# NSA attention of a fused two-layer network: mask on TensorE, exponential from PSUM, a pinned order two head pairs ahead

## The chip, the cores and the metric

The kernel runs on one core of a Trainium2 chip. TensorE (PE, with its weight loads PEld) multiplies matrices out of SBUF into PSUM; VectorE (DVE), ScalarE (ACT) and GpSimd (POOL) work on tiles; SyncE (SP) issues most of the DMAs. Each engine takes its instructions in the order of its own queue, and semaphores make one wait for another. The metric is the device time of one execution in microseconds (us).

## The reference, cut to what matters

The program is a network of width 1024 over 256 tokens: a mixer with retention and mLSTM, a feed-forward block, a gated embedding, then the NSA mixer (native sparse attention), a second feed-forward block and embedding, and two hybrid attention blocks. The change is in the NSA mixer, and in helpers that the hybrid blocks share with it. With 256 tokens all four selection blocks are selected and the window of 512 covers everything, so that the selected and the window branch are two causal attentions over all 256 keys, with keys and values of their own. What is computed per head and query:

```python
s = jnp.einsum('bghqd,bgnd->bghqn', qq, kc) * scale        # compressed branch: 15 block keys
p_c = jnp.where(cvalid, jax.nn.softmax(jnp.where(cvalid, s, NEG), axis=-1), 0.0)
o_cmp = jnp.einsum('bghqn,bgnd->bghqd', p_c, vc)
s = jnp.where(smask, einsum(qq, kg) * scale, NEG)          # selected branch
o_slc = einsum(softmax(s), vg)
s = jnp.where(wmask, einsum(qq, kwb) * scale, NEG)         # window branch
o_win = einsum(softmax(s), vwb)
return g[..., 0:1] * o_cmp + g[..., 1:2] * o_slc + g[..., 2:3] * o_win   # then @ w_out
```

There are 16 heads of 64 in two groups of 8; a group shares its keys and values.

## The kernel before, in words

Tokens stand in two blocks of 128 (`tb`), heads in pairs (`e` is the head in the pair), and a pair holds both branches (`b`: 0 selected, 1 window). There are eight pairs, four of each group.

The projections multiply fp32 by fp32 in three fp32r matmuls (`mm3`, L485 to L487): each operand is split into a high and a low half. `wt` loads a weight tile by SP, ACT casts the high half (L468, `whi`) and DVE takes the rest (L469, `wlo`), with four buffers of each kind. `nat` (L502) is a projection of 1024 columns deep, 512 wide, for both token blocks: 96 matmuls for two output halves, 48 for one query group.

The NSA stage goes: normalised input turned, compressed keys' and values' inputs, keys and values, gates, `compress(0)`, the queries of group 0 (`qgroup(0)`: projection, norm, query turn L1158), `compress(1)`, `qgroup(1)`, then `attention(0)` and `attention(1)`, then `nsa.out`, the output projection, which ends with the addition to the residual.

`attention` first does the compressed branch of the group, token block by token block: 4 small matmuls (L1172), a softmax of 9 DVE operations (L1178 to L1188) with one ACT exponential, a transpose (L1190) and a copy into `cT`. Then for each pair: per token block the scores `s4` (L1204), one matmul per head for both branches; per head and branch one DVE custom operation (L1207) that adds the mask, writes the masked scores to SBUF with their sign turned and takes the row extreme; the exponential on ACT from SBUF to SBUF with the row sum (L1209); reciprocal, gate, and 4 multiplications of the probabilities on DVE per token block (L1211 to L1216). `pv_pair` then transposes the probabilities, three 128x128 blocks into one PSUM bank (L703), copies them to a `pT` tile (ACT L708 or DVE L706), and multiplies with the values (L711, L714) onto the compressed part (L1218). The result is split into `xh` (ACT, L1222) and `xl` (DVE, L1223), the input of `nsa.out`.

PSUM has eight banks: three of `acc`, two of `sc`, two of `tp`, one of `po`. The order of the instructions on each engine is set by a scheduler that simulates the program as written and takes what is ready; in the stage before the change PE's order here is the scheduler's. `pinned()` (L436), used by the hybrid blocks, fixes PE's order to that in which the code is written; `high_priority` lets an operation go ahead of others in the scheduler's choice. A generator used as `fill` gives single steps of other work between.

Of the kernel before, what the change touches and what calls it, by code (L numbers as in the profile page):

```python
# [8 lines left out]
F32 = mybir.dt.float32  # L9
# [6 lines left out]
P = 128  # L16
# [357 lines left out]
class Builder:  # L374
# [318 lines left out]
    def pv_pair(self, po, p0, p1, v, ns, start):  # L693


        nc = self.nc
        for s in range(ns):
            pts = []
            for e in range(2):
                tp = self.pt.tile([P, 512], F32, tag="tp", name=self.nm("tp"))  # L700
                a0, a1 = p0(e, s), p1(e, s)
                for j, a in enumerate((a0, a1[:, 0:P], a1[:, P:T])):
                    nc.tensor.transpose(tp[:, j * P:(j + 1) * P], a, self.ident)  # L703
                pT = self.ph.tile([P, 384], F32, tag="pT", bufs=3, name=self.nm("pT"))
                if e:
                    nc.vector.tensor_copy(pT, tp[:, :384])  # L706
                else:
                    nc.scalar.activation(pT, tp[:, :384], AF.Copy)  # L708
                pts.append(pT)
            for e in range(2):  # L710
                nc.tensor.matmul(po[e * 64:e * 64 + 64, :], lhsT=v(s, 0, e), rhs=pts[e][:, 0:T],  # L711
                                 start=start and s == 0, stop=False)
            for e in range(2):
                nc.tensor.matmul(po[e * 64:e * 64 + 64, P:T], lhsT=v(s, 1, e), rhs=pts[e][:, T:384],  # L714
                                 start=False, stop=s == ns - 1)
# [287 lines left out]
    def nsa(self):  # L1003
# [56 lines left out]
        for b in range(2):  # L1060
            tp = self.pt.tile([P, 2, T], F32, tag="tp", name=self.nm("tp"))
            for g in range(2):
# [8 lines left out]
              for n, tags in (("k", [(a + b, 1) for b in "01" for a in ("qn", "qT")]),  # L1071
                              ("v", [("pr1", 2), ("pr1", 2), ("w1", 2), ("w1", 2)]))]
# [67 lines left out]
        def qgroup(g):  # L1140
            acc = self.nat(f"nsa.q{g}", xs, 8)
            qn = self.ph.tile([P, 2, 8, 64], F32, tag=f"qn{g}", name="qn")
            qT = self.ph.tile([P, 4, T], F32, tag=f"qT{g}", name="qT")
            a3 = lambda tb: acc[tb].rearrange("p (h d) -> p h d", d=64)
            for tb in range(2):
                if tb:
                    nc.scalar.activation(qn[:, tb], a3(tb), AF.Copy)
                else:
                    nc.vector.tensor_copy(qn[:, tb], a3(tb))
            qf = self.sm.tile([P, 2, 8], F32, tag="qf", name=self.nm("qf"))  # L1150
            head_factor(a3, 8, qf, 0.125)
            for tb in range(2):
                tt(qn[:, tb], qn[:, tb], qf[:, tb].unsqueeze(2).to_broadcast([P, 8, 64]), op=ALU.mult)
            for k0 in range(0, 4, 2):
# [6 lines left out]
                nc.scalar.activation(qT[:, k0:k0 + 2, :], tp, AF.Copy, scale=V("nsa_qg"))  # L1161
# [4 lines left out]
        def attention(g, qT):  # L1166

            cT = ph.tile([P, T], F32, tag="cpT", bufs=1, name="cpT")
            for tb in range(2):
                sp = self.psc.tile([P, 512], F32, tag="sc", name=self.nm("sc"))  # L1170
                for pr in range(4):
                    nc.tensor.matmul(sp[:, pr * 32:pr * 32 + 32], lhsT=qT[:, pr, tb * P:(tb + 1) * P], rhs=kc[:, g],  # L1172
                                     start=True, stop=True)
                e = ph.tile([P, 8, 16], F32, tag="ce", bufs=2, name=self.nm("ce"))
                mx = self.sm.tile([P, 8], F32, tag="cmx", name=self.nm("cmx"))
                fc = self.sm.tile([P, 8], F32, tag="cfc", name=self.nm("cfc"))
                b16 = lambda a: a.unsqueeze(2).to_broadcast([P, 8, 16])
                tt(e, sp[:, 0:128].rearrange("p (h n) -> p h n", n=16),  # L1178
                   c("nsa.cmask")[:, tb * 16:tb * 16 + 16].unsqueeze(1).to_broadcast([P, 8, 16]), op=ALU.add)
                nc.vector.tensor_reduce(mx, e, AX.X, ALU.max)  # L1180
                ts(mx, mx, -1e20, None, ALU.max)
                tt(e, e, b16(mx), op=ALU.subtract)
                nc.scalar.activation(e, e, AF.Exp)
                nc.vector.tensor_reduce(fc, e, AX.X, ALU.add)
                ts(fc, fc, 1e-30, None, ALU.max)
                nc.vector.reciprocal(fc, fc)
                tt(fc, fc, gate[:, tb, g * 8:g * 8 + 8, 0], op=ALU.mult)
                tt(e, e, b16(fc), op=ALU.mult)  # L1188
                tp = self.pt.tile([P, 2, T], F32, tag="tp", name=self.nm("tp"))
                nc.tensor.transpose(tp[:, 0, 0:P], e.rearrange("p h n -> p (h n)"), self.ident)  # L1190
                nc.scalar.activation(cT[:, tb * P:(tb + 1) * P], tp[:, 0, 0:P], AF.Copy)
            for pr in range(4):
                p1 = ph.tile([P, 2, 2, T], F32, tag="pr1", bufs=2, name=self.nm("pr1"))
                p0 = ph.tile([P, 2, 2, P], F32, tag="pr0", bufs=2, name=self.nm("pr0"))
                nm = self.sm.tile([P, 2, 2, 2], F32, tag="nm", name=self.nm("nmx"))
                l = self.sm.tile([P, 2, 2, 2], F32, tag="l", name=self.nm("l"))
                for tb, pt in ((1, p1), (0, p0)):
                    nk = P * (tb + 1)
                    banks = 2 if tb else 1
                    sps = [self.psc.tile([P, 512], F32, tag="sc", name=self.nm("sc")) for _ in range(banks)]  # L1200
                    for e in range(2):
                        hs = slice(e * 64, e * 64 + 64)
                        s4 = (sps[e] if tb else sps[0][:, e * 256:e * 256 + 256]).rearrange("p (b k) -> p b k", b=2)
# [7 lines left out]
                    nc.vector.reciprocal(l[:, tb], l[:, tb])  # L1211
                    hd = g * 8 + 2 * pr
                    tt(l[:, tb], l[:, tb], gate[:, tb, hd:hd + 2, 1:3], op=ALU.mult)
# [657 lines left out]
```

## Time and profile before

| | us |
|---|---|
| median of 3 runs | 1415.21 |
| lowest and highest | 1412.82, 1420.18 |
| profiled execution | 1417.63 |
| its span (first to last instruction) | 1415.8 |
| granted clock, mean over the span | 0.988 |

The profile is of one execution. Its busy times count an engine as busy while an instruction of it runs; since instructions overlap a little at their ends, the sum of single durations is larger than the busy time of their stretch. Times in the text are us from the start of the span. A granted clock of 1.00 is TensorE's level of 2.4 GHz and 0.50 is that of 1.2 GHz. Some matmul and other records are missing from the trace, so counts in a stretch fall short of those in the program by some per cent. The NSA stage runs from about 360 to 518.

### The profile page before, as it was taken

Reading aid. Unit: us, or ns where it says so; the run is one execution under the profiler, and the core shown is the slowest. Engines: PE = TensorE matmul, PEld = TensorE weight load, DVE = VectorE, ACT = ScalarE, POOL = GpSimd, SP = SyncE. Lnnn points to the kernel's source line nnn. Section 1 sums busy time; section 2 is a strip of 40 time slices with the busy share of each in tenths; the row PEclk is TensorE's granted clock in tenths of the full one; section 3 lists DMA queues with packets and bytes.
Section 4 is the critical chain, followed back from the end, with each engine's and each line's share of the span. In section 5 each row is a group of like instructions: output and inputs, shape, how many; then the busy total and the mean of one; then the engine's idle time right before and its main releaser. Section 6 shows DMA issues by size and latency. Waiting matters only on the chain. (4 is left out here: it accounts for less than half of the span.)

```text
span 1415.8 us, 23842 instructions
## 1 busy us (share of the span) xinstructions
PE 1371.8 (97%) x9029; PEld 1196.3 (84%) x9029; DVE 1019.5 (72%) x2215; ACT 761.0 (54%) x1383; POOL 70.9 (5%) x108
## 2 busy tenths in 40 slices
PE   8999999999899999999999999999999999999997
PEld 8777999888765589998779898997879998997886
DVE  6777889887777778888587777555577767546467
ACT  6355656536455656554365656445555555545443
POOL 0000000003000000000030202000000201000000
PEclk9999999999997999999999999999999999999999
DMA  6444667896640047668754444453665544554562
GB/s 246 149 144 158 183 228 242 294 332 221 226 150 16 28 152 238 213 234 315 242 169 155 150 148 136 158 172 116 196 205 171 151 137 127 158 184 133 171 194 75
DMA packets 74759, 251.90 MB, mean 178 GB/s; under 512 B 10578, under 2 KB 14162, under 8 KB 74516
## 3 DMA queue, kind: packets, MB, share of 16 engines
q1 hardware_dynamic: 68880, 239.87, 50.9%
q0 software_dynamic: 4272, 7.17, 2.3%
q10 hardware_dynamic: 1492, 3.34, 0.8%
q8 instruction: 71, 1.16, 0.3%
q14 instruction: 44, 0.36, 0.1%
HBM read 248.42 MB, written 1.90 MB: 177 GB/s over the span
## 5 line engine op out<-in xcount | busy, mean ns | idle before, releaser
L469 DVE TENSOR_TENSOR wlo<-raw,whi 128x1024 fp32r<-128x1024 f32 (+2 forms) x386 | 461.6, 1199 | 212.6 <-ACT whi L468 211.9
L468 ACT ACTIVATE whi<-raw 128x1024 fp32r<-128x1024 f32 (+2 forms) x386 | 399.3, 1036 | 330.5 <-PE acc L487 146.9
L485 PE MATMUL acc<-xh,whi 128*128 128x256 f32 (+1 forms) x1360 | 390.1, 288 | 7.5 <-ACT xh L601 5.0
L486 PE MATMUL acc<-xl,whi 128*128 128x256 f32 (+1 forms) x1360 | 386.0, 284 | 0.3 <-DVE xl L602 0.3
L487 PE MATMUL acc<-xh,wlo 128*128 128x256 f32 (+1 forms) x1360 | 385.0, 283 | 0.5 <-DVE wlo L469 0.5
L485 PEld LDWEIGHTS acc<-xh,whi 128*128 128x128 f32 (+1 forms) x1360 | 258.7, 191 | 14.9 <-ACT xh L601 6.0
L486 PEld LDWEIGHTS acc<-xl,whi 128*128 128x128 f32 (+1 forms) x1360 | 259.4, 191 | 1.9 <-DVE xl L602 1.1
L487 PEld LDWEIGHTS acc<-xh,wlo 128*128 128x128 f32 (+1 forms) x1360 | 259.3, 191 | 1.7 <-DVE wlo L469 0.8
L485 PE MATMUL acc<-whi,xh 128*128 128x512 f32 (+2 forms) x688 | 251.5, 367 | 2.0 <-ACT xh L601 0.8
L487 PE MATMUL acc<-whi,xl 128*128 128x512 f32 (+2 forms) x688 | 248.8, 363 | 1.4 <-DVE xl L602 1.4
L486 PE MATMUL acc<-wlo,xh 128*128 128x512 f32 (+2 forms) x688 | 247.9, 361 | 0.0
L485 PEld LDWEIGHTS acc<-whi,xh 128*128 128x128 f32 x688 | 130.0, 189 | 24.6 <-ACT xh L601 2.2
L487 PEld LDWEIGHTS acc<-whi,xl 128*128 128x128 f32 x688 | 129.9, 189 | 22.4 <-DVE xl L602 2.6
L486 PEld LDWEIGHTS acc<-wlo,xh 128*128 128x128 f32 x688 | 130.1, 189 | 18.7 <-issue 1.7
L485 PE MATMUL acc<-whi,gh 128*128 128x512 f32 x176 | 70.3, 399 | 0.0
L486 PE MATMUL acc<-wlo,gh 128*128 128x512 f32 x176 | 69.5, 395 | 0.0
L487 PE MATMUL acc<-whi,gl 128*128 128x512 f32 x176 | 69.4, 394 | 0.0
L1526 POOL DMA_DIRECT2D bias<-brow x48 | 29.2, 635 | 448.2 <-DVE nmx L1551 157.6
L625 ACT ACTIVATE sqj<-h 128x512 f32<-128x512 f32 (+1 forms) x40 | 23.5, 587 | 48.8 <-DVE h L1783 16.3
L1333 DVE CUSTOM_DVE_ANT_0 adw<-adw,ada 128x1024 f32<-128x1024 f32 x32 | 39.1, 1221 | 13.1 <-DMA adw<-weights 13.1
L951 DVE SCALAR_TENSOR_TENSOR cy<-zp,vecs,cy 128x256 f32<-128x256 f32 x88 | 42.2, 480 | 0.8
L485 PEld LDWEIGHTS acc<-whi,gh 128*128 128x128 f32 x176 | 33.1, 188 | 8.1 <-issue 0.5
(423 smaller groups left out, 1871.2 us busy)
## 6 DMA issues: line engine op xcount, KB each, us to landing
raw<-weights SPq DMA_DIRECT2D x384, 512.0 KB, 3.9
adw<-weights SPq DMA_DIRECT2D x48, 512.0 KB, 4.8
bias<-brow POOLq DMA_DIRECT2D x48, 128.0 KB, 3.8
w<-weights SPq DMA_DIRECT2D x8, 512.0 KB, 7.7
raw<-weights SPq DMA_DIRECT2D x8, 416.0 KB, 3.7
const_ab<-consts SPq DMA_DIRECT2D x1, 1536.0 KB, 6.9
h<-x SPq DMA_DIRECT2D x4, 256.0 KB, 4.5
gb<-rows ACTq DMA_DIRECT2D x2, 512.0 KB, 5.1
```

The lines of the kernel that those rows point to most:

```text
L468: nc.scalar.activation(hi, r, AF.Copy)
L469: nc.vector.tensor_tensor(lo, r, hi.bitcast(F32), op=ALU.subtract)
L485: mm(out, lhsT=a[0], rhs=b[0], start=start, stop=False)
L486: mm(out, lhsT=a[0], rhs=b[1], start=False, stop=False)
L487: mm(out, lhsT=a[1], rhs=b[0], start=False, stop=stop)
L625: self.nc.scalar.activation(j, src, AF.Square, scale=2048.0 ** -0.5, accum_out=dst)
L951: stt(y, az[:, k:k + T], V(f"ffn_cw{i}", k * 22 + j), y, ALU.mult, ALU.add)
L1333: nc.vector.tensor_tensor_reduce(raw, raw, cr, 1.0, 0.0, ALU.mult, ALU.add, m[:, j:j + 1])
L1526: nc.gpsimd.dma_start(b3[:, g], bass.AP(b0.tensor, b0.offset + ((4 * qd + 2 * pr + e) * 3 + g) * 384 + 127, [[24 * 384 - 16, 8], [24 * 384 ...
```

## The change

In the NSA stage:

- The mask is added by TensorE: `idr`, an identity, and `tri`, the 128x128 triangle of the mask, both cast to fp32r on ACT once. Four matmuls of `idr` with `tri` a pair add to the diagonal blocks of the scores in PSUM. Two casts on ACT are new, with a wait for the NSA constants.
- DVE takes the row maximum of each score bank with one `tensor_reduce` per head and token block (four a pair), and ACT takes the exponential straight from PSUM into the probability tile `pr` (three buffers). The custom operation is gone.
- The scores of both heads of a pair stand next to each other on PE, those of token block 0 in two `acc` banks.
- The probabilities are transposed and copied back in place (`turn_block`), and all value matmuls of a pair come together (`pv_all`); both were helpers of the hybrid blocks and are now shared. Their copies there now have priority.
- The compressed branch takes both token blocks in one bank, with ten DVE operations a group, eight of them of double width.
- The query projection is split: `q_in` (first token block 0, then 1), `q_norm`, `q_turn`. Its second group's second token block is filler around the first pairs' scores; the query turn of group 1 comes between pairs.
- PE's order from the query turn of group 0 to the last pair is pinned: the scores of pair n+2 come ahead of the transposes of pair n.

The diff, cut to its core:

```diff
+    def turn_block(self, a, on_vector):
+        tp = self.pt.tile([P, 512], F32, tag="tp", name=self.nm("tp"))
+        for j in range(3):
+            nc.tensor.transpose(tp[:, j * P:(j + 1) * P], a[:, j * P:(j + 1) * P], self.ident)
+        with self.tc.high_priority(offset=200):
+            if on_vector:
+                nc.vector.tensor_copy(a, tp[:, :384])
+            else:
+                nc.scalar.activation(a, tp[:, :384], AF.Copy)
+    def pv_all(self, items, start=True):
+        mm = self.nc.tensor.matmul
+        for n, (po, pts, v) in enumerate(items):
+            for e in range(2):
+                mm(po[e * 64:e * 64 + 64, :], lhsT=v(0, e), rhs=pts[e][:, 0:T], start=start and n == 0, stop=False)
...
-                        nc.tensor.matmul(s4, lhsT=qT[hs, pr, tb * P:(tb + 1) * P], rhs=kT[hs, g, :, 0:nk],
-                                         start=True, stop=True)
-                        for b in range(2):
-                            nc.vector.tensor_tensor_reduce(pt[:, e, b], s4[:, b], mask[:, T - nk:], -1.0, 3e38, ALU.add,
-                                                           ALU.min, nm[:, tb, e, b:b + 1])
-                            nc.scalar.activation(pt[:, e, b], pt[:, e, b], AF.Exp, scale=-1.0, bias=nm[:, tb, e, b:b + 1],
-                                                 accum_out=l[:, tb, e, b:b + 1])
...
+        idr, tri = [ph.tile([P, P], F32R, tag=t, name=t) for t in ("idr", "tri")]
+        nc.scalar.activation(idr, self.ident, AF.Copy)
+        nc.scalar.activation(tri, mask[:, P:T], AF.Copy)
+        def scores(g, pr, qT):
...
+            for tb in (1, 0):
+                nk = P * (tb + 1)
+                for e in range(2):
+                    hs = slice(e * 64, e * 64 + 64)
+                    nc.tensor.matmul(sps[tb][e], lhsT=qT[hs, pr, tb * P:(tb + 1) * P], rhs=kT[hs, g, :, 0:nk],
+                                     start=True, stop=False)
+            for tb in (1, 0):
+                for e in range(2):
+                    nc.tensor.matmul(sps[tb][e][:, :, P * tb:P * tb + P], lhsT=idr,
+                                     rhs=tri.unsqueeze(1).to_broadcast([P, 2, P]), start=False, stop=True)
+            for tb in (1, 0):
+                o, nk = P * tb, P * (tb + 1)
+                for e in range(2):
+                    nc.vector.tensor_reduce(nm[:, tb, e], sps[tb][e], AX.X, ALU.max, negate=True)
+                    for b in range(2):
+                        nc.scalar.activation(pp[:, e, b, o:o + nk], sps[tb][e][:, b], AF.Exp, bias=nm[:, tb, e, b:b + 1],
+                                             accum_out=l[:, tb, e, b:b + 1])
...
+        self.take(q_in(0, qn[0]), 9)
+        q_norm(0, qn[0])
+        fill = q_in(1, qn[1])
+        compress(1)
+        self.take(fill, 4)
+        with self.pinned():
+            qT, cT = [q_turn(0, qn[0])], []
+            self.take(fill, 1)
+            es = compressed(0, qT[0])
+            pps = [scores(0, 0, qT[0])]
+            self.take(fill, 2)
+            pps.append(scores(0, 1, qT[0]))
+            self.take(fill, 2)
+            with self.tc.high_priority(offset=200):
+                q_norm(1, qn[1])
+            cT.append(compressed_turn(es))
+            for n in range(8):
+                g, pr = divmod(n, 4)
+                if n < 6:
+                    pps.append(scores((n + 2) // 4, (n + 2) % 4, qT[(n + 2) // 4]))
+                if n == 1:
+                    qT.append(q_turn(1, qn[1]))
+                values(g, pr, pps.pop(0), cT[g], fill)
+                if n == 1:
+                    es = compressed(1, qT[1])
+                if n == 2:
+                    cT.append(compressed_turn(es))
```

How the order of the engines changes is shown at three places. On PE in the loop over pairs, before (`sc` are score banks, `tp` the transposes' banks, `po` the output bank, `pr_802` and `pr_803` the two probability tiles of one pair):

```order
L1204 MATMUL sc_4916<-kT,qT 128x512
L703 MATMUL tp_4835<-const_g,pr_803_4795 128x128
L703 MATMUL tp_4835<-const_g,pr_802_4794 128x128 x2
L703 MATMUL tp_4841<-const_g,pr_803_4795 128x128
L703 MATMUL tp_4841<-const_g,pr_802_4794 128x128 x2
L1204 MATMUL sc_4917<-kT,qT 128x512
L711 MATMUL po_4833<-pT_4839,vsw 64x256
L711 MATMUL po_4833<-pT_4845,vsw 64x256
L714 MATMUL po_4833<-pT_4839,vsw 64x128
L714 MATMUL po_4833<-pT_4845,vsw 64x128
L703 MATMUL tp_4851<-const_g,pr_803_4795 128x128
L703 MATMUL tp_4851<-const_g,pr_802_4794 128x128 x2
```

The scores of later banks stand singly between transposes and value matmuls of the pair before, and each branch's values follow its transposes at once. On PE in the same loop in the changed kernel (`acc` are here the score banks of token block 0):

```order
L1234 MATMUL sc_4953<-kT,qT 128x512
L1234 MATMUL sc_4954<-kT,qT 128x512
L1234 MATMUL acc_4951<-kT,qT 128x256
L1234 MATMUL acc_4952<-kT,qT 128x256
L1238 MATMUL sc_4953<-tri,idr 128x2x128
L1238 MATMUL sc_4954<-tri,idr 128x2x128
L1238 MATMUL acc_4951<-tri,idr 128x256
L1238 MATMUL acc_4952<-tri,idr 128x256
L704 MATMUL tp_4987<-const_g,pr_4801 128x128 x3
L704 MATMUL tp_4992<-const_g,pr_4801 128x128 x3
L704 MATMUL tp_4997<-const_g,pr_4801 128x128 x3
L704 MATMUL tp_5002<-const_g,pr_4801 128x128 x3
```

All four score matmuls and the four mask matmuls of a pair stand in a block ahead of the twelve transposes of the pair two before, and the eight value matmuls of that pair follow these.

On DVE in the loop over pairs, before (`nmx` the row extremes, `l` the row sums, `pT` the copies of transposed probabilities):

```order
L706 COPY pT_4711<-tp_4707 128x384
L1207 ISA pr_802_4794,nmx_4796<-sc_4798,const_nsa 128x256
L1207 ISA nmx_4796 128x1
L1211 RECIPROCAL l_4722<-l_4722 128x4
L1207 ISA pr_802_4794,nmx_4796<-sc_4798,const_nsa 128x256
L1207 ISA nmx_4796 128x1
L1213 TENSOR_TENSOR l_4722<-l_4722,gate 128x4
L1207 ISA pr_802_4794,nmx_4796<-sc_4799,const_nsa 128x256
L1207 ISA nmx_4796 128x1
L1216 TENSOR_SCALAR pr_787_4720<-pr_787_4720,l_4722 128x128 x3
L1223 TENSOR_TENSOR xl_4198<-po_4683,xh_4197 128x256
L1216 TENSOR_SCALAR pr_787_4720<-pr_787_4720,l_4722 128x128
```

The operations of two pairs are mixed as they become ready. On DVE in the same loop in the changed kernel (`pr` is copied to in place):

```order
L1243 TENSOR_REDUCE nmx_4949<-sc_4953 128x2
L1243 TENSOR_REDUCE nmx_4949<-sc_4954 128x2
L708 COPY pr_4801<-tp_4992 128x384
L1243 TENSOR_REDUCE nmx_4949<-acc_4951 128x2
L1243 TENSOR_REDUCE nmx_4949<-acc_4952 128x2
L708 COPY pr_4801<-tp_5002 128x384
L1247 RECIPROCAL l_4950<-l_4950 128x4
L1249 TENSOR_TENSOR l_4950<-l_4950,gate 128x4
L1253 TENSOR_SCALAR pr_4948<-pr_4948,l_4950 128x256 x4
L1247 RECIPROCAL l_4950<-l_4950 128x4
L1249 TENSOR_TENSOR l_4950<-l_4950,gate 128x4
L1267 TENSOR_TENSOR xl_4198<-po_5007,xh_4197 128x256
```

A pair now takes four maxima, two copies, and two rounds of reciprocal, gate and multiplications; `xl` of the pair that is being finished stands between the second round's gate and its multiplications.

On PE at the start of the attention, before:

```order
L485 MATMUL acc_4413<-whi_4469,xh_3890 128x512
L486 MATMUL acc_4413<-wlo_4470,xh_3890 128x512
L487 MATMUL acc_4413<-whi_4469,xl_3891 128x512
L1111 MATMUL sc_4402<-raw_4400,cmpu_4393 30x64 x2
L1172 MATMUL sc_4527<-kcb,qT 128x32 x4
L1132 MATMUL tp_4407<-vcn,const_nsa 128x64
L1172 MATMUL sc_4548<-kcb,qT 128x32 x4
L1132 MATMUL tp_4407<-vcn,const_nsa 128x64
L1204 MATMUL sc_4573<-kT,qT 128x512
L1204 MATMUL sc_4574<-kT,qT 128x512
L1204 MATMUL sc_4591<-kT,qT 128x256
```

The second query group's 48 matmuls are done ahead of the first score of group 0. On PE at the same place in the changed kernel:

```order
L487 MATMUL acc_4404<-whi_4442,xl_3891 128x512
L1173 MATMUL tp_4455<-const_g,qn 128x128 x4
L1138 MATMUL tp_4399<-vcn,const_nsa 128x64
L1173 MATMUL tp_4461<-const_g,qn 128x128 x4
L485 MATMUL acc_4467<-whi_4406,xh_3890 128x512
L486 MATMUL acc_4467<-wlo_4407,xh_3890 128x512
L487 MATMUL acc_4467<-whi_4406,xl_3891 128x512
L485 MATMUL acc_4467<-whi_4406,xh_3890 128x512
L486 MATMUL acc_4467<-wlo_4407,xh_3890 128x512
L487 MATMUL acc_4467<-whi_4406,xl_3891 128x512
L1188 MATMUL acc_4474<-kcb,qT 128x32 x8
L1234 MATMUL sc_4502<-kT,qT 128x512
```

Token block 0 of the second query group (24 matmuls) comes ahead of the query turn of group 0 (L1173), six matmuls of token block 1 follow it, and then come the compressed scores (L1188) and the first pair's scores.

On ACT the two casts (`idr`, `tri`) stand among the copies of the turned input at the start of the stage, behind the third of the stage's `xh` copies (L601). In the hybrid blocks the instructions are the same; at four places a copy of transposed probabilities on ACT stands ahead of an exponential that it stood behind, and at two places on DVE a copy moves ahead of one operation. The queues of POOL and SP have the same instructions in the same order.

## Rows read from the trace of the kernel before

**Rows 1.** The page: span, and busy time of each engine.
```profile
span 1415.8 us, 23842 instructions
...
PE 1371.8 (97%) x9029; PEld 1196.3 (84%) x9029; DVE 1019.5 (72%) x2215; ACT 761.0 (54%) x1383; POOL 70.9 (5%) x108
```

**Rows 2.** Stretch, length, busy of PE, PEld, DVE, ACT, POOL, PEclk, DMA.
```profile
412.00:419.20 7.20, 6.73 (x40) 5.17 (x40) 4.09 (x10) 5.16 (x10) 0.00 (x0) 1.00 0.51 155
419.20:439.70 20.50, 18.86 (x46) 9.08 (x47) 15.45 (x81) 9.71 (x33) 0.00 (x0) 0.50 0.15 49
440.00:504.00 64.00, 63.86 (x337) 36.47 (x335) 46.81 (x224) 36.95 (x134) 0.00 (x0) 1.00 0.08 26
505.00:516.00 11.00, 11.00 (x50) 9.11 (x49) 8.90 (x11) 7.10 (x12) 0.00 (x0) 1.00 0.68 229
```

**Rows 3.** Timeline of PE, first score and last output matmul: start, length.
```profile
420.61 1.22 PE L1204 MATMUL sc<-kT,qT 64*128 64x512 f32 x1
...
516.05 0.39 PE L487 MATMUL acc<-whi,xl 128*128 128x512 f32 x1
```

**Rows 4.** The high halves of the eight pairs' outputs on ACT, line L1222.
```profile
L1222 ACT ACTIVATE xh<-po x8: 359/384/385, 443.4 to 504.0; 128x256 fp32r<-128x256 f32 x8
```

**Rows 5.** Timeline of PE: single matmuls of several shapes.
```profile
354.00 0.28 PE L485 MATMUL acc<-whi,xh 128*128 128x256 f32 x1
354.12 0.28 PE L486 MATMUL acc<-wlo,xh 128*128 128x256 f32 x1
...
461.95 1.12 PE L1204 MATMUL sc<-kT,qT 64*128 64x512 f32 x2
463.00 0.87 PE L703 MATMUL tp<-const_g,pr 128*128 128x128 f32 x6
...
856.78 1.13 PE L1546 MATMUL sc<-qk,qk 64*128 64x256 f32 x8
```

**Rows 6.** DVE by line from 440 to 504: count, busy, mean ns, idle before.
```profile
L1207 DVE CUSTOM_DVE_ANT_0 pr<-sc,const_nsa 128x128 f32<-128x128 f32 (+1 forms) x50 | 16.1, 345 | 1.3 <-PE tp L703 0.8
L1216 DVE TENSOR_SCALAR pr<-pr,l 128x128 f32<-128x128 f32 (+1 forms) x55 | 14.3, 313 | 0.1
L706 DVE COPY pT<-tp 128x384 f32<-128x384 f32 x15 | 8.3, 556 | 9.6 <-PE tp L703 9.5
...
L469 DVE TENSOR_TENSOR wlo<-raw,whi 128x1024 fp32r<-128x1024 f32 x3 | 3.6, 1216 | 0.7 <-ACT whi L468 0.7
L1223 DVE TENSOR_TENSOR xl<-po,xh 128x256 fp32r<-128x256 f32 x7 | 3.0, 425 | 3.1 <-ACT xh L1222 3.0
```

**Rows 7.** The maxima and sums of the norms, line L1020: shortest, median, longest ns.
```profile
L1020 DVE TENSOR_REDUCE qf<-sqj x4: 664/680/686, 402.2 to 419.6; 128x8 f32<-128x512 f32 x4
L1020 DVE TENSOR_REDUCE kf<-sqj x2: 412/414/415, 383.3 to 386.3; 128x4 f32<-128x256 f32 x2
```

**Rows 8.** Timeline of DVE at the norm of query group 0.
```profile
409.65 0.18 DVE L1026 SCALAR_TENSOR_TENSOR qf<-hf,rs 128x16 f32<-128x16 f32 x1
409.86 1.29 DVE L1153 TENSOR_TENSOR qn<-qn,qf 128x512 f32<-128x512 f32 x2
```

**Rows 9.** Timeline of ACT at the start of the NSA stage.
```profile
360.39 0.35 ACTq L419 DMA_DIRECT2D const_nsa<-consts  x1
...
364.96 0.84 ACT L601 ACTIVATE xh<-tp,vecs 128x256 fp32r<-128x256 f32 x2 [2.75 <-PE tp L597]
```

**Rows 10.** DMA issues: KB of one, us from issue to landing.
```profile
const_nsa<-consts ACTq DMA_DIRECT2D x1, 291.0 KB, 4.6
```

**Rows 11.** Three more stretches, columns as in rows 2.
```profile
129.08:132.49 3.41, 1.96 (x13) 1.53 (x12) 3.41 (x10) 3.41 (x5) 0.00 (x0) 1.00 0.13 41
357.78:361.19 3.41, 0.87 (x4) 0.78 (x5) 2.31 (x8) 1.45 (x5) 0.16 (x1) 1.00 0.07 22
361.20:364.60 3.40, 3.40 (x12) 2.69 (x12) 2.31 (x11) 1.01 (x4) 0.00 (x0) 0.50 0.91 277
```

**Rows 12.** Timeline of PE inside the first of them.
```profile
129.78 1.03 PE L597 MATMUL tp<-const_g,h 128*128 128x128 f32 x8
```

More of the change, by code (lines that the diff above doesn't have):

```diff
@@ L691, in half_of, with take @@
         return o
-    def pv_pair(self, po, p0, p1, v, ns, start):
-        nc = self.nc
-        for s in range(ns):
-            pts = []
-            for e in range(2):
[L700 to L709, printed above, removed]
-            for e in range(2):
[L711 to L715, printed above, removed]
+    @staticmethod
+    def take(gen, n):
+        for _ in range(n):
+            next(gen, None)
+    def turn_block(self, a, on_vector):
+        nc = self.nc
+        tp = self.pt.tile([P, 512], F32, tag="tp", name=self.nm("tp"))
[9 more added lines that the diff above has]
+        for n, (po, pts, v) in enumerate(items):
+            for e in range(2):
+                mm(po[e * 64:e * 64 + 64, :], lhsT=v(0, e), rhs=pts[e][:, 0:T], start=start and n == 0, stop=False)
+        for n, (po, pts, v) in enumerate(items):
+            for e in range(2):
+                mm(po[e * 64:e * 64 + 64, P:T], lhsT=v(1, e), rhs=pts[e][:, T:384], start=False,
+                   stop=n == len(items) - 1)
     def load_x(self, c):
@@ L1182, in attention @@
[L1182 to L1190, printed above, removed]
@@ new lines, in compressed, with compressed_turn @@
+            return e
+        def compressed_turn(e):
+            cT = ph.tile([P, T], F32, tag="cpT", bufs=2, name="cpT")
+            tp = self.pt.tile([P, 2, T], F32, tag="tp", name=self.nm("tp"))
+            for tb in range(2):
+                nc.tensor.transpose(tp[:, 0, tb * P:(tb + 1) * P], e[:, tb].rearrange("p h n -> p (h n)"), self.ident)
+            with self.tc.high_priority(offset=200):
+                nc.scalar.activation(cT, tp[:, 0], AF.Copy)
+            return cT
+        idr, tri = [ph.tile([P, P], F32R, tag=t, name=t) for t in ("idr", "tri")]
@@ new lines, in values @@
+        def values(g, pr, pp, cT, fill):
+            for e in range(2):
+                for b in range(2):
+                    self.turn_block(pp[:, e, b], b)
+                self.take(fill, 1)
+            po = self.pv.tile([P, T], F32, tag="po", name=self.nm("po"))
+            nc.tensor.matmul(po, lhsT=vc[:, g, 2 * pr:2 * pr + 2].rearrange("p h d -> p (h d)"), rhs=cT,
+                             start=True, stop=False)
+            self.pv_all([(po, [pp[:, e, b] for e in range(2)], lambda kb, e, b=b: vsw[:, kb, b, g, :])
+                         for b in range(2)], False)
+            nc.scalar.activation(oh[:, 4 * g + pr], po, AF.Copy)
+            tt(ol[:, 4 * g + pr], po, oh[:, 4 * g + pr].bitcast(F32), op=ALU.subtract)
@@ L1225, in nsa @@
         compress(0)
-        q0 = qgroup(0)
+        qn = [self.ph.tile([P, 2, 8, 64], F32, tag=f"qn{g}", name="qn") for g in range(2)]
+        self.take(q_in(0, qn[0]), 9)
+        q_norm(0, qn[0])
+        fill = q_in(1, qn[1])
         compress(1)
-        q1 = qgroup(1)
-        attention(0, q0)
-        attention(1, q1)
+        self.take(fill, 4)
+        with self.pinned():
+            qT, cT = [q_turn(0, qn[0])], []
+            self.take(fill, 1)
+            es = compressed(0, qT[0])
[3 more added lines that the diff above has]
+            self.take(fill, 2)
+            with self.tc.high_priority(offset=200):
+                q_norm(1, qn[1])
[11 more added lines that the diff above has]
+                    cT.append(compressed_turn(es))
@@ L1487, in quad_in @@
                 yield
[L1489 to L1491 removed]
         def probs():
             return ph.tile([P, 3, 384], F32, tag="pr", bufs=4, name=self.nm("pr"))
[L1498 to L1515 removed]
+        turn, pv_all, take = self.turn_block, self.pv_all, self.take
         def quad(qd, fill):
```

119 lines of the change are left out of this document (51 added, 68 removed).

## The prediction

> **What bounds the kernel now.** I read the page first: PE is busy for 1371.8 of 1415.8 us [rows 1], so over the whole program only PE's work and PE's gaps matter. Then the stages, with the table of stretches [rows 2], because the change sits in one of them. The reader is to see four things there. From 412 to 419.2 PE ends the second query group. From 419.2 to 439.7 the granted clock is 0.50, that is 1.2 GHz: the attention begins cold. From 440 to 504 the clock is 1.00 and PE is busy for 63.86 of 64.00 us, while DVE has 46.81 and ACT 36.95: the pairs are PE-bound. From 505 to 516 only output matmuls are left, fifty records in 11.00 us with PE never idle. The timeline gives the ends: first score matmul at 420.61, last output matmul from 516.05 to 516.44 [rows 3]. The eight outputs appear from 443.4 to 504.0 [rows 4], one per (504.0 - 443.4)/7 = 8.66 us. In that pace stand the 46 or so output matmuls that the scheduler put between (96 in all, some 50 after 505).
>
> **The change on PE.** Removed: scores that run one after the other. One 512-column score matmul takes 463.00 - 461.95 = 1.05 us (its two records), so two of them and two of 256 columns (half, 0.53) cost up to 3.15 a pair. Where two heads of 64 rows stand next to each other, the hybrid block shows four 256-column matmuls, eight records, in 1.13 us [rows 5], against 4 x 0.53 = 2.1 one by one: neighbours run side by side. The order puts all four scores of a pair next to each other, so 1.05 + 0.53 = 1.6, a gain of 1.5 at most. Added: four mask matmuls of 256 columns in fp32r; two such follow each other by 354.12 - 354.00 = 0.12 [rows 5], so 4 x 0.12 = 0.5. The transposes (12) and value matmuls (8) stay. PE's net is about -1 a pair. Before, a pair without the output matmuls cost (64.0 - 43 x 0.22)/7.4 = 7.4 us, 43 being the output matmul records of that stretch and 0.22 = 11.00/50 the price of one alone [rows 2]; after, about 6.3, and less if the clumsy changes of shape in the old order cost something: 5.5 to 6.4. The output matmuls that leave the loop are not saved: they come later.
>
> **The change on DVE.** Removed per pair: eight custom operations, 8 x 16.1/50 = 2.6, with eight reads of the accumulator beside them. Added: four maxima over banks of 512 and 256 columns, priced by reduces over the same counts, 2 x 0.680 + 2 x 0.414 = 2.19 [rows 7]; those read SBUF and these PSUM, so I allow 0 to 0.1 more each. Left: eight multiplications at 14.3/55 = 0.26, 2.08; two copies at 0.556, 1.11; `xl` 0.43 [rows 6]; two reciprocals and two gates at about 0.17 as the small operations of the norm [rows 8], 0.68. Sum 6.5 a pair. So DVE, not PE, sets the pace after: 6.5 against 5.5 to 6.4. Its queue is in order, and `xl` now stands ahead of the last four multiplications; it waits for the value matmuls, then ACT's `xh`. Behind it wait those multiplications, the next pair's maxima, and so ACT's exponentials and the scores two pairs on, which need the two `sc` banks. I put 0.2 a pair for that (bounds 0 and 1.5: nothing where the values end first, and the whole of a value block, `xh` and `xl` where they do not). I take 6.7 a pair.
>
> **ACT** has eight exponentials from PSUM instead of SBUF, and the copies; at 36.95 of 64 [rows 2] and a faster loop it has about 36.95/64 x 8.66 = 5.0 us a pair, under DVE's. It is cover, not path.
>
> **The sum.** Start: by the new order only half of the second query group stands ahead of the query turn of group 0, so the turn waits for `qn`, whose multiplications end at 409.86 + 1.29 = 411.15 [rows 8]. Eight transposes take 1.03 [rows 12], six filler matmuls 6 x 0.22 = 1.3 beside the copies of the turn, and I allow 1.0 for the rest of the copies and the compressed scores: first scores at 414.5. Before: 420.6 [rows 3]. The remaining 18 filler matmuls fall beside DVE's first maxima. End of the loop: eight pairs at 6.7 make 53.6; DVE also does two compressed blocks (ten operations, mostly 256 columns wide, estimate 2.5 each, from 0.414 for 256 columns and 0.17 for the small [rows 7, 8]), the norm of group 1 (2 x 0.68 + 1.29 + twelve at 0.17 = 4.7), and four low halves of the output weights (4 x 1.216 = 4.9 [rows 6]) plus two multiplications of 512 columns for the compressed values, 1.4 as the reduces over 512: 16. From 414.5 plus 0.8 for the first scores that is 414.5 + 0.8 + 53.6 + 16.0 = 484.9; with 2.6 for the ramps at both ends, where the pairs stand alone, 487.5; before, the last pair ended at 504.0 + 0.38 = 504.4 [rows 4]. Then the output projection: only about 11 of its 96 matmuls stand between the last pairs in the new order, so 85 x 0.22 = 18.7, where 50 stood before: end at 506.2 against 516.44, 10.2 earlier. So of the 17 us by which the pairs end earlier, 7 are given back, since the output matmuls had filled PE's queue between pairs and now come behind.
>
> Against it: the cast `tri` waits on ACT for the NSA constants, issued at 360.39 and landing 4.6 later, so 365.0 [rows 9, 10], and behind it stand `xh` copies that began at 364.96 and on which the first projections wait: the two casts, at most 0.42 each (two of 256 columns in 0.84), put them 0.3 to 0.9 later; I take 0.5, since the first cast does not wait. The hybrid blocks' six moved copies I cost at nothing: PE there has other matmuls in its queue; without that cover each would move its pair by one copy, 0.56, either way; I keep -1 to +1. Behind the NSA stage everything is the same work on a full PE, so what the stage gains the end gains. Total: -10.2 + 0.5 = -9.7. The profiled execution's 1417.63 becomes 1408; that execution is 2.4 above the median of its runs, 1415.21, to which I apply the same difference: 1405.5, rounded to **1406**.
>
> **What the clock could do.** In the old cold spell of 20.5 us DVE was busy for 15.45 [rows 2], so at full clock it could have been 5 shorter at most. The new order makes PE's start at 409 to 425 thin: transposes, narrow compressed matmuls, waits. In the stretch 129.08 to 132.49 PE was busy for 1.96 of 3.41 us, eight transposes in it and a wait, and the clock stayed at 1.00; in 357.78 to 361.19 it was busy for 0.87, and the stretch behind is at 0.50 [rows 11, 12]. One thin stretch passed, another did not. The Trainium skill (TensorE: Matmul & The Clock Gate, Part 4: PE-mode transpose) says that transposes do not count as busy for the clock in the same way; by it the new loop, a quarter of whose PE time is transposes, would run cold and the time be that of rival D. The trace does not bear this out: the stretch at 129.08, whose PE work is half transposes and then a wait, kept the full clock.
>
> **Rivals.**
>
> B, cold again: the clock falls as before around the first pairs. For: the start is thin, and before it fell at the same place. At 1.2 GHz PE's 5.5 to 6.4 a pair become 11 to 12.8, 4 to 6 over DVE's pace; one spell as long as the old one covers two pairs, in whose time DVE has the norm and the compressed block to do as well, so 3 to 6 lost: -9.7 + 4.5 = -5.2, 1410.
>
> C, the in-order queues: each pair pays the full 1.5 for `xl` and its like, 8 us a pair: 1.3 x 8 = 10.4 on -9.7, 1416. For: one output bank `po`, two `sc` banks and in-place copies tie pair n+2 to pair n; DVE already waited 9.5 for the transposes and 3.0 for `xh` in 64 us [rows 6]. Against: the same form of loop leaves scores two pairs ahead as cover.
>
> D, slower: the clock falls and stays, because a DVE-paced loop leaves PE idle a part of each pair. At 1.2 GHz a pair costs 11.9, 5.2 more than 6.7. Two cold pairs eat the gain (10.4); seven make -9.7 + 36.4 = +27, 1442. It decides from the third cold pair. By the rule of the Trainium skill above this would be the case. Against: at half speed PE is busy all the time, which before was followed by full speed at 440 [rows 2].
>
> E, more than forecast: no ramps, DVE operations overlapping at their ends so that a pair takes 6.2: another 4 to 6: -9.7 - 5 = -14.7, 1400.5.
>
> **How the numbers follow.** Forecast 0.45, its own range 1403 to 1409; E 0.13; B 0.21; C 0.13; D 0.08. About 0.5%, 7 us, is what a measurement of this kernel can tell from no change, so faster means below 1408.1: nearly all of E, four fifths of the forecast, little of B: 0.54. Same takes the rest of the forecast, B and most of C: 0.36. Slower is D and a bit of C: 0.10. For 8 in 10, E's lower half and D are left out: 1398 to 1417.
>
> **What would show it.** First score (L1234) near 414.5; `xh` of the eight pairs 6.5 to 7 apart and PE with gaps in the loop that DVE ends; last `xh` near 487; some 85 output matmuls behind it in 19 us; clock 1.00 in most of 415 to 487. Wrong if pairs are 8 apart (C), if the clock is 0.50 for more than one spell (D), or if the score records of the two heads do not overlap (PE then 7 and more a pair). Outside 360 to 510 no stage should differ by over 1 us.

## The result

The changed kernel takes 1402.39 us (median of 6 runs, 1400.03 to 1403.77), the kernel before 1415.31 (6 runs). The ratio is 0.990 with a 95% interval of 0.988 to 0.992: 12.9 us faster by the medians, where 9.7 was forecast. The two profiled executions are 15.9 apart (1417.63 and 1401.72), since that of before lies above its median. From the last block sum of `compress(1)` (the matmuls of L1092 before, L1098 after, which end at 402.9 and 402.4) to the last output matmul (516.44 and 501.11) the traces give 113.57 us before and 98.75 after, 14.8 less; behind that they have 899.4 and 898.8. So the gain is where it was looked for.

A part of it goes with the clock. Each run lists its mean granted clock: 0.992 to 0.998 in the six runs of the changed kernel, 0.984 to 0.992 in the 43 runs of the kernel before that stand beside the experiments. Among these 43 the time follows it: ten runs at 0.986 or less have a median of 1418.3, eight at 0.990 or more one of 1413.2, about 1 us for 0.001. The two kernels' means lie 0.006 apart (0.994 and 0.988), so by estimate some 5 of the 12.9 us go with the clock. This is no experiment on the clock: the runs only show that the two move together.

The page, then the stretches and the outputs `xh` of the kernel after (columns as in [rows 2]):

```profile
span 1399.9 us, 23775 instructions
...
PE 1353.6 (97%) x9061; PEld 1192.5 (85%) x9061; DVE 1013.8 (72%) x2101; ACT 759.1 (54%) x1383; POOL 70.5 (5%) x108
```

```profile
412.00:416.00 4.00, 3.76 (x28) 3.46 (x28) 0.93 (x2) 2.52 (x4) 0.00 (x0) 1.00 0.00 0
416.00:434.00 18.00, 16.63 (x80) 10.32 (x82) 17.55 (x56) 13.57 (x46) 0.00 (x0) 1.00 0.28 89
434.00:464.00 30.00, 26.39 (x183) 16.87 (x179) 27.87 (x97) 19.19 (x79) 0.00 (x0) 1.00 0.06 19
464.00:481.00 17.00, 16.89 (x132) 11.83 (x132) 12.30 (x41) 9.75 (x40) 0.00 (x0) 1.00 0.00 1
481.00:501.00 20.00, 20.00 (x92) 16.44 (x89) 12.10 (x16) 11.42 (x16) 0.00 (x0) 1.00 0.58 196
```

```profile
L1266 ACT ACTIVATE xh<-po x8: 384/414/446, 434.6 to 481.2; 128x256 fp32r<-128x256 f32 x8
```

The attention runs at clock 1.00; the cold stretch of [rows 2] is gone. Outputs run from 434.6 to 481.2, where before it was 443.4 to 504.0 [rows 4]. Between 416 and 464 DVE is nearly full and PE has some idle time; from 464 PE is full. From 481 only output matmuls are left, 92 records in 20.0 us, against the fifty of before.

One pair on PE after, start and length, from its scores to the next pair's:

```profile
446.78 1.13 PE L1234 MATMUL sc<-kT,qT 64*128 64x512 f32 x4
447.75 0.60 PE L1234 MATMUL acc<-kT,qT 64*128 64x256 f32 x4
448.27 0.51 PE L1238 MATMUL sc<-tri,idr 128*128 128x256 f32 x2
448.62 0.40 PE L1238 MATMUL acc<-tri,idr 128*128 128x256 f32 x2
448.85 0.82 PE L704 MATMUL tp<-const_g,pr 128*128 128x128 f32 x6
450.17 0.55 PE L704 MATMUL tp<-const_g,pr 128*128 128x128 f32 x3 [0.50 <-ACT pr L710]
451.33 0.55 PE L704 MATMUL tp<-const_g,pr 128*128 128x128 f32 x3 [0.61 <-DVE pr L708]
451.72 0.60 PE L1262 MATMUL po<-cpT,vcb 128*128 128x256 f32 x2
452.24 1.08 PE L717 MATMUL po<-pr,vsw 128*64 128x256 f32 x8
453.16 0.61 PE L720 MATMUL po<-pr,vsw 128*64 128x128 f32 x8
453.69 0.44 PE L1214 MATMUL tp<-const_g,ce 128*128 128x128 f32 x2
454.06 0.70 PE L1234 MATMUL sc<-kT,qT 64*128 64x512 f32 x2
```

The four 512-column score records, two for each head, take 447.75 - 446.78 = 0.97, where one head alone took 1.05 before [rows 5]: the two heads run side by side. Scores and masks take 2.07. The transposes wait twice for in-place copies. The last line starts the next pair (the view ends within it). This pair takes 7.28, with the compressed block's work on DVE beside it, the three behind it 6.1 to 6.3.

The same loop on DVE, one pair from its first maximum:

```profile
455.98 1.29 DVE L1243 TENSOR_REDUCE nmx<-sc 128x2 f32<-128x512 f32 x2
457.18 0.55 DVE L708 COPY pr<-tp 128x384 f32<-128x384 f32 x1
457.64 0.75 DVE L1243 TENSOR_REDUCE nmx<-acc 128x2 f32<-128x256 f32 x2
458.37 0.56 DVE L708 COPY pr<-tp 128x384 f32<-128x384 f32 x1
459.39 0.18 DVE L1247 RECIPROCAL l<-l 128x4 f32<-128x4 f32 x1 [0.46 <-ACT pr L1245]
459.60 0.17 DVE L1249 TENSOR_TENSOR l<-l,gate 128x4 f32<-128x4 f32 x1
459.80 1.14 DVE L1253 TENSOR_SCALAR pr<-pr,l 128x256 f32<-128x256 f32 x4
460.86 0.17 DVE L1247 RECIPROCAL l<-l 128x4 f32<-128x4 f32 x1
461.07 0.17 DVE L1249 TENSOR_TENSOR l<-l,gate 128x4 f32<-128x4 f32 x1
461.15 0.42 DVE L1267 TENSOR_TENSOR xl<-po,xh 128x256 fp32r<-128x256 f32 x1
461.48 0.87 DVE L1253 TENSOR_SCALAR pr<-pr,l 128x128 f32<-128x128 f32 x4
```

The next pair's first maximum starts at 462.26, so this pair takes 6.28, with 5.71 busy and 0.46 of waiting for ACT's exponentials; the next takes 6.08, with 5.70 busy and 0.27 of that wait. Two maxima take 1.20 from start to the next operation, though a single one lasts 0.686 (mean of 16): successive operations overlap at their ends.

### The profile page after: what moved, and what is told of

It reads as the page before. It is cut to its first block, busy times and chain, and to the rows that moved or that the text cites. A ratio compares the mean times of both kernels' runs of the same rounds, so it can differ in the third digit from the quotient of the medians.

```text
span 1399.9 us, 23775 instructions
## 1 busy us (share of the span) xinstructions
PE 1353.6 (97%) x9061; PEld 1192.5 (85%) x9061; DVE 1013.8 (72%) x2101; ACT 759.1 (54%) x1383; POOL 70.5 (5%) x108
## 4 chain that ended last, share of the span: by engine, by line
PE 80%; DVE 9%; DMA 4%; ACT 4%; issue 2%; POOL 1%; SPq 0%; DVEq 0%; ACTq 0%; POOLq 0%
PE acc L485 23%; PE acc L486 22%; PE acc L487 22%; DVE wlo L469 3%; DMA raw<-weights 3%; PE tp L704 2%; PE po L717 2%; ACT whi L468 1%; PE sc L1696 1%; PE po L720 1%; PE sc L1590 1%; DMA gb<-rows 1%; PE tp L1436 1%; DVE pr L1253 0%; PE tp L597 0%
## 5 line engine op out<-in xcount | busy, mean ns | idle before, releaser
L704 PE MATMUL tp<-const_g,pr 128*128 128x128 f32 x336 | 49.6, 278 | 6.6 <-ACT pr L710 4.6
L704 PEld LDWEIGHTS tp<-const_g,pr 128*128 128x128 f32 x336 | 37.4, 141 | 15.9 <-ACT pr L710 9.2
```

The costliest lines, as they stand in the source:

```text
L704: nc.tensor.transpose(tp[:, j * P:(j + 1) * P], a[:, j * P:(j + 1) * P], self.ident)
```

## The experiments

All ratios are to runs of the kernel before on the same chip; the changed kernel itself stands at ratio 0.990 [0.988, 0.992]. The medians of the kernel before beside the experiments are 1415.7 to 1416.2, so that differences from the changed kernel are given by medians; where they are 3.2 us or less, the two intervals overlap. Distances of outputs are those between starts of `xh`.

**More work on DVE.**

```diff
+        junk = ph.tile([P, 256], F32, tag="junk", name="junk")
...
+                for b in range(2):
+                    ts(junk, kT[:, 0, b], l[:, tb, 0, 0:1], None, ALU.mult)
```

> The changed kernel with four more DVE multiplications of 256 columns a pair (two a token block, on data that nobody reads, each behind the row sums of its pair). Such a multiplication takes 0.27 when it follows another (four in 1.14), so 1.07 us a pair, 8.5 us in all. Theory 1 (DVE with its in-order queue paces the pairs): DVE was busy for 57.7 of the 65.7 us from the first score to the last pair's end, most of its idle time in the last two pairs, so the last pair ends 4.5 to 8.5 later and so does the kernel. Theory 2 (PE paces the pairs, DVE only follows): the extra work falls into DVE's idle time, 0 to 1.5 later.

Measured: ratio 0.997 [0.996, 0.999], 1412.8, some 10 later than the changed kernel: more than either theory allows. The loop's stretch:

```profile
440.00:480.00 40.00, 32.96 (x196) 21.64 (x196) 34.19 (x120) 22.23 (x92) 0.00 (x0) 0.84 0.04 14
```

The granted clock is 0.84 there, and neither engine is full. Four stretches at 0.50, 20.4 us in all, lie between 429 and 481, where the changed kernel has none. So the price of DVE's work cannot be read from the 10: two outputs with a cold stretch between them are 2.0 to 3.5 further apart than in the changed kernel, two with none 0.1 (8.70 against 8.56), and two with only the last 1.0 us of one 0.65 (6.93 against 6.28). The added work is 1.07 a pair, so that at full clock it is partly hidden. This run alone does not decide between the theories, and that the added work brought the cold stretches on is not shown.

**More work on PE.**

```diff
-            for tb in (1, 0):
-                for e in range(2):
-                    nc.tensor.matmul(..., stop=True)
+            for rep in range(3):
+                for tb in (1, 0):
+                    for e in range(2):
+                        nc.tensor.matmul(..., stop=rep == 2)
```

> The changed kernel with each mask matmul done three times (the mask is so large that the result stays): eight more fp32r matmuls of 256 columns a pair at 0.115, 0.92 us of PE a pair, 7.4 in all. Theory 2 (PE paces the pairs): 5 to 7.4 later. Theory 1 (DVE paces them): PE was idle for 5 of 48 us from 416 to 464, so 0 to 3 later, more than 0 only because scores then come later to DVE in the first pairs.

Measured: 0.998 [0.997, 1.000], 1413.1, again over 10 later, against theory 1. So PE's work is not hidden either:

```profile
440.00:470.00 30.00, 27.59 (x201) 19.29 (x202) 24.84 (x90) 18.42 (x78) 0.00 (x0) 1.00 0.01 2
```

At this full clock outputs are 7.0 apart, where it was 6.1 to 6.3: the added 0.9 is paid nearly in full. Ahead of the first output, which came 7.0 later after `compress(1)`, this run has a cold stretch too (432.8 to 439.6), so that the total is not the matmuls' price alone. A third theory is argued from these lines: in the loop PE (26.4 of 30.0) and DVE (27.9) are both nearly full and wait for each other in turn, so work added to either lengthens each pair.

**The mask back on DVE.**

```diff
-                    nc.tensor.matmul(sps[tb][e][:, :, P * tb:P * tb + P], lhsT=idr, ...)
-                    nc.vector.tensor_reduce(nm[:, tb, e], sps[tb][e], AX.X, ALU.max, negate=True)
+                        nc.vector.tensor_tensor_reduce(a, sps[tb][e][:, b], mask[:, T - nk:], -1.0, 3e38, ALU.add, ...)
```

> The changed kernel with the mask and the row maximum given back to DVE's custom operation (eight a pair, 0.42 and 0.28 with the accumulator read, 2.8 us, for four reduces, 2.0 to 2.2) and the exponential from SBUF; the four mask matmuls are gone. Pinned order, filler, compressed branch and value matmuls stay. Theory 1 (DVE paces): +0.6 to 0.8 a pair, 4 to 6 us later. Theory 2 (PE paces): four matmuls fewer a pair, 2 to 3.7 us earlier. If the gain of the change came from the order alone, within 1 of the changed kernel.

Measured: 0.991 [0.989, 0.993], 1403.5: the same as the changed kernel. Mask by TensorE and exponential from PSUM bring nothing that shows. In the middle two pairs are 0.8 and 1.1 longer, somewhat over theory 1's price, and DVE is full while PE is not:

```profile
448.00:464.00 16.00, 11.13 (x82) 6.83 (x82) 15.78 (x75) 10.70 (x42) 0.00 (x0) 1.00 0.18 66
```

but the first output comes 2.5 earlier after `compress(1)`. The seven pairs behind it take 48.0 instead of 46.6, and the output matmuls end 1.2 earlier.

**PE's order left to the scheduler.**

```diff
-        with self.pinned():
+        with nullcontext():
```

> The changed kernel with PE's order left to the scheduler instead of being pinned; all operations stay. Theory 1 (DVE paces, the order on PE only has to keep it fed): -1 to +3. Theory 2 (the block of scores two pairs ahead on PE is where the gain comes from): 5 to 10 later, with output matmuls and single score matmuls between the pairs again.

Measured: 0.993 [0.991, 0.995], 1405.6, 3.2 later by the medians, between the prices of the two theories. The scheduler again puts most pairs' scores of the two heads apart (0.56 of busy time a 512-column record, as in the kernel before, 0.34 in the changed kernel) and breaks up the value matmuls (0.22 a 256-column record, 0.14 in the changed kernel), and PE is the full engine:

```profile
440.00:470.00 30.00, 29.55 (x174) 18.06 (x174) 23.77 (x80) 18.55 (x72) 0.00 (x0) 1.00 0.06 19
```

So nearly 10 of the 12.9 us remain without the neighbour order in most pairs. Much of the PE time that the neighbours save seems to be waiting time in the changed kernel, where PE is busy for 26.39 of 30.00.

**The heads' scores apart.**

```diff
                     nc.tensor.matmul(sps[tb][e], lhsT=qT[hs, pr, ...], rhs=kT[hs, g, :, 0:nk], start=True, stop=False)
-            for tb in (1, 0):
-                for e in range(2):
                     nc.tensor.matmul(sps[tb][e][:, :, P * tb:P * tb + P], lhsT=idr, ...)
```

> The changed kernel with each score matmul followed at once by its own mask matmul, so that the two heads' scores no longer stand next to each other on PE; the same operations otherwise. If neighbours run side by side, this costs 1.05 + 0.53 = 1.6 us of PE a pair. Theory 3 (both engines nearly full): 8 to 13 later. If DVE alone paced the pairs: 0 to 3. If the heads did not run side by side in the changed kernel: 0.

Measured: 1.005 [1.003, 1.008], 1423.2: slower than the kernel before, 20.8 behind the changed one. One pair's scores and masks:

```profile
462.39 1.12 PE L1234 MATMUL sc<-kT,qT 64*128 64x512 f32 x2
463.45 0.39 PE L1236 MATMUL sc<-tri,idr 128*128 128x256 f32 x1
463.76 1.12 PE L1234 MATMUL sc<-kT,qT 64*128 64x512 f32 x2
464.81 0.38 PE L1236 MATMUL sc<-tri,idr 128*128 128x256 f32 x1
465.13 0.70 PE L1234 MATMUL acc<-kT,qT 64*128 64x256 f32 x2
465.75 0.38 PE L1236 MATMUL acc<-tri,idr 128*128 128x256 f32 x1
466.07 0.70 PE L1234 MATMUL acc<-kT,qT 64*128 64x256 f32 x2
```

They take 467.07 - 462.39 = 4.68 instead of 2.07, 2.6 a pair. The score matmuls take 3.35 of it from start to start, where they took 1.49: 1.9 more, and 1.6 was expected. The masks between them take 0.31 to 0.38 each, 1.33 in all, where the four took 0.58 together: 0.75 more. PE is full:

```profile
440.00:480.00 40.00, 39.18 (x187) 23.67 (x188) 29.82 (x101) 20.80 (x82) 0.00 (x0) 0.87 0.08 27
```

Of the single edits this one costs most, but the 20.8 are not the price of the order alone. Four stretches at clock 0.50, 17.0 us in all, lie between 415 and 471, where the changed kernel has none, and the mean clock of the eight runs is 0.987 against 0.994. Behind 472, at full clock, the outputs are twice 8.4 apart, where they were 6.1 and 6.3: 2.1 to 2.3 a pair. The edit also does more than undo the neighbours: between any two of them there now stands a full-row mask matmul, which the kernel before does not have.

**The second query group first.**

```diff
-        self.take(fill, 4)
+        self.take(fill, 8)
```

> The changed kernel with the second query group's second token block (24 matmuls, 5.4 us of PE) done ahead of the query turn of group 0, as in the kernel before, instead of around the first two pairs' scores. Theory 3 (in the loop PE and DVE are both nearly full, 5.9 and 5.6 of 6.1 us a pair, and what was gained ahead of the first output, 8.3 of the stage's 14.9, comes from starting DVE's work earlier beside a PE that stays busy): the first score comes 4 later and the first output 2 to 4 later; if the thin stretch that is then left sends the clock to 0.50 as in the kernel before, 5 to 9 later. Rival (the start does not matter, the loop does): 0 to 1.

Measured: 0.993 [0.991, 0.994], 1404.8, 2.4 later. The first score came 3.9 later after `compress(1)`, the first output 8.0 later. Of this 3 is won back up to the second output (8.0 behind the first instead of 10.7); ahead of it DVE no longer has the second group's norm to do, which ends at 425.5 instead of 439.4. The thin stretch and what followed:

```profile
416.00:422.90 6.90, 3.51 (x23) 2.45 (x23) 5.79 (x21) 4.00 (x10) 0.00 (x0) 1.00 0.51 163
422.90:436.60 13.70, 12.28 (x37) 7.28 (x36) 10.84 (x42) 6.55 (x33) 0.00 (x0) 0.50 0.00 1
```

The cold stretch is back, 13.7 us long; the 4 us by which the first output is later still than the first score lie beside it. So the query matmuls around the first scores do two things, and the clock is one of them.

**One pair ahead.** `scores` of pair n+1 instead of n+2 ahead of pair n.

> The changed kernel with the scores one pair ahead instead of two, the order pinned as it is written. Then the maxima, exponentials and multiplications of pair n+1 have only the transposes and values of pair n beside them on PE. Theory 3: PE waits for the multiplications in each pair, 1 to 2.5 us a pair, 7 to 18 later. Rival (one pair is enough cover): within 2.

Measured: 0.990 [0.988, 0.992], 1402.0: no difference. Theory 3 expected 7 to 18 and was wrong here; the second pair of cover is not used.

**The casts of identity and triangle.**

```diff
+        with self.tc.issue_after(self.last_xh):
             nc.scalar.activation(idr, ...); nc.scalar.activation(tri, ...)
```

> The changed kernel with the two casts of identity and triangle queued on ACT behind the last copy of the turned input, so that no such copy waits for the NSA constants. Theory: PE's wait of 1.79 us for the input copies (at 362 to 364 of the changed kernel) is the casts' price, so 1.5 to 1.8 earlier. Rival: the next copies wait for something else anyway (transposes, weights) and it is 0 to 0.5.

In the changed kernel PE waits for the copies behind `tri`:

```profile
361.63 0.39 PE L485 MATMUL acc<-whi,xh 128*128 128x512 f32 x1
363.80 0.39 PE L485 MATMUL acc<-xh,whi 128*128 128x256 f32 x1 [1.79 <-ACT xh L601]
```

Measured without: 0.991 [0.989, 0.993], 1402.0, no difference. The wait is gone, but the stretch ahead of it was at half clock in the profiled execution, as in the kernel before [rows 11]; in the changed kernel's trace such a stretch lies at 390 to 394:

```profile
359.00:362.50 3.50, 3.28 (x9) 2.79 (x10) 3.36 (x13) 1.41 (x5) 0.16 (x1) 0.51 0.58 153
```

The rival's price stands; its reason is not shown.

**The output weights' casts later.** The casts of four tiles (`wt`) queued behind the sixth pair's scores.

> The changed kernel with the casts of the first half's output weights (ACT high halves, DVE low halves, four tiles) queued behind the scores of the sixth pair instead of among the first pairs. In the changed kernel three or four of DVE's casts (1.2 each, 4.8) stand at 426 to 437, where DVE has no idle time, and it is idle for 4.7 us from 464 to 481. Theory 1 (DVE paces): the first outputs come 3 to 4.8 earlier, the end 2 to 4 earlier. Rival: the casts then delay the last pairs and the output matmuls, 0 to 2 later.

Measured: 0.991 [0.989, 0.992], 1403.2, no difference. The output matmuls ended 1.2 later after `compress(1)`. The first output came 1.1 later, with 3.4 us at half clock ahead of it, the second 0.7 earlier, the sixth 2.2 later: what the second pair gains, the later ones pay.

**Both.** 

> Both edits together: the casts of identity and triangle behind the input copies, and the casts of the output weights behind the sixth pair's scores. If both theories hold, 3.5 to 5.5 earlier than the changed kernel; if neither, within 1.

Measured: 0.989 [0.988, 0.991], 1401.7: no difference from the changed kernel.

**The kernel before, kept busy.**

```diff
+                    if g == 0:
+                        nc.tensor.matmul(wm[:, 0:T], lhsT=qT[:, pr, tb * P:(tb + 1) * P], rhs=qT[:, 0], start=True, stop=True)
```

> The kernel before with eight matmuls of 256 columns in fp32 (0.53 us each at full clock, 4.2 in all, results not read) between the narrow compressed matmuls of the first group, nothing else changed. It asks what the stretch of 20.5 us at clock 0.50 costs there. If the clock then stays at 1.00 and the cold stretch is what holds the first pair: the first output comes at 438 to 441 instead of 443.4, the kernel 2 to 5 earlier. If DVE holds it there (it is busy for 15.45 of the 20.5 us): first output at 441 to 446 and the time within 3 of the kernel before, up to 4 later.

Measured: 1.006 [1.005, 1.008], 1424.4. The cold stretch was not prevented; it came later and was longer:

```profile
416.00:427.10 11.10, 8.77 (x43) 5.62 (x42) 8.72 (x42) 5.19 (x12) 0.00 (x0) 1.00 0.41 140
427.10:454.40 27.30, 26.03 (x67) 12.00 (x67) 13.22 (x70) 11.96 (x44) 0.00 (x0) 0.50 0.00 0
```

So this run does not price the cold stretch of the kernel before, and that price stays open.

**DVE's mask in the outer pairs only.** Custom operation for pairs 0, 1, 6 and 7, mask matmuls for 2 to 5.

> The changed kernel with DVE's masking operation and the exponential from SBUF for the first two and the last two pairs, and mask matmuls with the exponential from PSUM for the four between. With DVE's mask in all pairs the first output came 2.6 us earlier and the last pairs were 1 us closer together, while the pairs between were 0.6 us longer. If these add up, 2 to 4 earlier than the changed kernel; if not, within 1.5.

Measured: 0.993 [0.991, 0.995], 1405.3, 2.9 later by the medians: the parts do not add up. Why is open; the trace's stage is only 0.7 longer than the changed kernel's, the rest lies behind it, and the mean clock of its runs is 0.990 against 0.994. None of these kernels beats the changed one beyond the noise.

## Why the prediction was right, and where it was off

The direction was right, and so was the overlap of the heads: both heads' 512-column scores take 0.97, where one took 1.05. The prediction put the pair on PE at 5.5 to 6.4 us; in the middle the pairs are 6.1 to 6.3 apart with PE busy for 5.8. A part of PE's saving is not in the sum, which left the value matmuls as they were. They stand in one block now and cost less, by these lines 0.24 and 0.15 us of busy time a record before, 0.14 and 0.08 after:

```profile
L711 PE MATMUL po<-pT,vsw 128*64 128x256 f32 x62 | 15.1, 405 | 0.1
L714 PE MATMUL po<-pT,vsw 128*64 128x128 f32 x63 | 9.6, 278 | 0.0
...
L717 PE MATMUL po<-pr,vsw 128*64 128x256 f32 x64 | 8.7, 392 | 0.0
L720 PE MATMUL po<-pr,vsw 128*64 128x128 f32 x64 | 4.9, 273 | 0.0
```

The first two lines are from 440 to 504 before, the others from 415.9 to 481.6 after. That the neighbours on PE are the cause of the 12.9 is not shown. Setting masks between them costs 20.8, but partly at a lower clock; leaving the order to the scheduler, which parts most of them, costs 3.2. No run undoes the value block or the joint compressed block alone, so how the gain divides among the edits stays open.

The time itself was partly luck. 1402.4 lies just outside the forecast's own range, 1403 to 1409, and nearer to case E (1400.5) than to 1406. In the stage 14.8 were gained where 10.2 were forecast, and the sum has no term for the clock, with which some 5 of the 12.9 go.

Step by step: the first score was forecast at 414.5 and came at 415.9. The output tail was put at 18.7 and took 19.5. The hybrid blocks were put at nothing, and the time behind the stage changed by 0.6. `tri` was put at 0.5; PE waits 1.8 there, and removing the wait gave nothing that shows.

The step that was mis-sized is the end of the loop, 487.5, which came at 481.6. Two terms of that sum were wrong. DVE's pair was summed from single durations to 6.5, with 0.2 added for its in-order queue; back to back the same operations take 5.7 busy, 6.1 to 6.3 with the wait. And all eight pairs got that price and 2.6 for ramps on top, while the last two, which have no scores to share DVE with, are 4.1 to 4.2 apart and paced by PE (busy for 16.89 of 17.00 from 464). "DVE, not PE, sets the pace" was half right: work added on PE is paid nearly in full at full clock, work added on DVE in part.

Rival B (a cold start) did not happen in the profiled execution, but it is near: with the query matmuls moved away it returned. Rival C (8 a pair) did not: the first two distances are 10.7 and 8.6, with the second group's norm and compressed block on DVE, the next three 6.1 to 6.8. Rival D did not: the loop ran at 1.00 with its transposes in it. The loop with extra DVE work was granted 0.84 and cost 10 us, but the run with the heads apart was granted 0.87 with PE full (39.18 of 40.00), so that D's reason, idle time on PE, is not shown. Case E had the right cause (overlapping ends, a pair of 6.2) and was too unlikely in the forecast.

By place, the 14.8 are 8.3 ahead of the first output (earlier first score 4.2; the rest beside the vanished cold stretch) and 6.5 in the seven pairs and the output matmuls behind them. With the second query group first, 8.0 of the 8.3 come back at the first output, and 5.0 are left at the end of the stage.

## What to carry to other kernels

Put matmuls that use half the rows next to each other in the order, and keep others from coming between: here a pair's scores and masks took 2.07 us that way and 4.68 the other. Then ask what the engine does with the time saved; here much of it seems to have become waiting. Price an engine that will be full by the distance of starts in a back-to-back stretch, not by the sum of listed durations. Before crediting the headline edit of a change, undo it alone: here the mask on TensorE was worth nothing that shows. And set the granted clocks of two runs beside each other before a difference is put down to an edit: part of several prices here goes with the clock.

## What the runs showed of the hardware

A mask matmul of 256 columns that stands between two 64-row matmuls costs 0.31 us (heads apart); four in a row cost 0.58 together (changed kernel). A maximum over a PSUM bank of 512 costs DVE 0.686, as a reduce of that width from SBUF did (0.680 [rows 7]). Loops with PE busy for 32.96 and 39.18 of 40 us were granted 0.84 and 0.87 of the clock, one with 26.39 of 30 was granted 1.00: here the busy share of a stretch does not tell its clock.
